# The first stage of a two-block transformer: modulation products in quarters of the array's columns, x times norm on VectorE, another order of weights

## The chip, the cores and the metric

The kernel runs on one core of a Trainium2 chip. The metric is the device time of one execution in microseconds (us), the median of several. The core has TensorE (PE in the rows: matrix products, with its weight loads as PEld), VectorE (DVE), ScalarE (ACT) and GpSimd (POOL); SyncE (SP) only starts transfers here. Each engine works through its own instructions in order, and waits at one of them until what it reads is there and what it writes is free.

## The reference

Everything is fp32. Two transformer blocks on 512 rows of width 1024 follow each other. The change is in the first few lines of the first block, where the input is normalised and modulated before any projection:

```python
m  = jax.nn.silu(c) @ w_mod[l] + b_mod[l]          # c: 1 x 1024, w_mod: 1024 x 6144
sh1, sc1, g1, sh2, sc2, g2 = jnp.split(m, 6, axis=-1)
mc = jax.nn.silu(c_ctx) @ w_mod[l] + b_mod[l]      # the same weights, the context's vector
csh1, csc1, ... = jnp.split(mc, 6, axis=-1)
h  = rms_norm(x, norm1_g[l])  * (1.0 + sc1)  + sh1  # 512 x 1024
hc = rms_norm(xc, norm1_g[l]) * (1.0 + csc1) + csh1 # 256 x 1024
gq, gk, gv, nq, nk, nv, fu, cu, gl = jnp.split(h @ w_in, PROJ_SPLITS, axis=-1)
```

`h` feeds all projections of the token mixer (a convolution branch from `cu`, a Fourier branch from `fu`, a neighbourhood attention from `nq, nk, nv`, a grouped attention), then come a mixture of experts and the second block, which the change does not touch.

## The kernel before, in words

Activations lie transposed: 1024 features as 8 chunks k of 128 partitions, 512 rows in the free dimension. A large product is made in three passes so that it keeps fp32 accuracy: ScalarE casts a raw weight tile (`wraw`, 512 KB) to `whi`, VectorE makes `wlo` = raw - hi, and TensorE adds hi*hi, lo*hi and hi*lo. A projection job of 128 output columns is 8 chunks times 3 matmuls = 24 matmuls of 128x512.

The first stage, in `mixers` (from line 934) and the functions it starts, does this:

- `silu_c` makes silu of the two vectors c and c_ctx (`csil`, and its hi and lo parts `cparts`).
- `jobs_mod`/`mod_job`: the 2048 columns of w_mod that hold shift and scale are 4 groups g of 512; each group comes in 4 transfers kq (`mraw`, 512 KB, two chunks k each). The first transfer of a group is multiplied as it is (native fp32, two matmuls, which the trace shows as four records); the other three are split into `mod_hi` (ScalarE) and `mod_lo` (VectorE) and multiplied in four matmuls each against `cparts`. At the end of a group VectorE copies the sum from the bank to `m`, four small matmuls by `pairs` turn it into columns, and VectorE adds the bias and forms `A` = (1 + scale) * gain. Event `mod0` to `mod3` then stands for group 0 to 3; group g serves the chunks 2g and 2g+1 of h.
- `modulated`: squares and sums of x, the reciprocal root (`xr`), a broadcast over partitions by four transposes, a copy of it to `xbc` on ScalarE, and x times `xbc` on GpSimd chunk by chunk. `modulated_chunk` then makes `h_hi` and `h_lo` of a chunk with that chunk's `A` and shift on ScalarE and VectorE. The same function makes `hc` from ctx.
- `conv_first` is the first projection: three weights `win` (units of the convolution branch) are worked on together, two chunks k of each in turn, 72 matmuls. After it come five more jobs of the convolution, then the Fourier branch's first job.

The order of all instructions comes from a scheduler written in Python. Each piece of work is a generator that names the engine that it wants next and what it needs; `Net.run` always takes the piece that a modelled clock says can start first, with a small bonus for its priority. Transfers of a `stream` are issued ahead as far as a ring of raw tiles reaches. In `mixers` three streams are queued one after the other: `mod_a` (groups 0 and 1, 8 transfers), `jobs0` (the three `win` weights, behind a hold until mod_a's transfers are issued), and `mod_b` (groups 2 and 3, behind a hold until those of jobs0 are). They share one ring of 6 raw tiles. All instructions are recorded by one helper, so the line in the rows is L341 everywhere, and tiles are told apart by their names.

Later in the block, `modulation_rest` computes the other 4096 columns of `m` on VectorE, a multiply-add (`macc`) for each half of a 256 KB transfer (`mw`); its pieces stand between the neighbourhood attention's, whose value tiles `nv` come back from DRAM in 18 transfers on SP's queue.

Of the kernel before, what the change touches and what calls it, by code (L numbers as in the profile page):

```python
# [196 lines left out]
PE, ACT, DVE, POOL, SP = "pe", "act", "dve", "pool", "sp"  # L197
# [191 lines left out]
class Net:  # L389
# [345 lines left out]
    def silu_c(self):  # L735

        nc = self.nc
        self.csil = self.keep.tile([128, 8, 4], F32, name="csil")
        nc.gpsimd.memset(self.csil, 0.0)
        self.cparts = self.keep.tile([128, 8, 4], F32R, name="cparts")  # L740
        self.pairs = self.keep.tile([4, 2], F32, name="pairs")
        self.mod1 = self.keep.tile([128, 16, 2], F32, name="mod1")
        self.A1 = self.keep.tile([128, 8, 2], F32, name="A1")
        self.mod2 = self.keep.tile([128, 4, 8], F32, name="mod2")
        cv = self.vec("cvec").rearrange("p (k c) -> p k c", k=8)
        yield ACT, cv
        c = self.csil[:, :, :2]
        nc.scalar.activation(c, cv, AF.Tanh, scale=0.5)
        yield DVE, c
        nc.vector.scalar_tensor_tensor(c, c, 1.0, cv, op0=OP.add, op1=OP.mult)  # L750
        nc.vector.tensor_scalar(c, c, 0.5, None, op0=OP.mult)
        nc.vector.tensor_tensor(self.pairs, self.ident[:4, :2], self.ident[:4, 2:4], op=OP.add)
        yield from self.split(self.cparts[:, :, 0:2], self.cparts[:, :, 2:4], c)
        self.mark("cparts", self.cparts, c)

    def jobs_mod(self, a, after=None):
        if after:
            yield [], partial(self.hold, after)
        for g in range(2 * a, 2 * a + 2):
            for kq in range(4):  # L760
                yield [(self.T["wmod1"][g, kq], 2, 512, kq == 0)], partial(self.mod_job, g, kq)

    def mod_job(self, g, kq, w):

        nc = self.nc
        if kq == 0:
            yield PE, self.banks, "cparts"
            self.modp = self.banks.take()
        p = self.modp
        for k in range(2):  # L770
            for z, v in enumerate(w):
                c = self.csil if len(w) == 1 else self.cparts
                nc.tensor.matmul(p[:4, :], c[:, kq * 2 + k], v[:, k], start=kq + k + z == 0,
                                 stop=(kq, k, z) == (3, 1, len(w) - 1))
        if kq < 3:
            return
        yield TAIL
        yield DVE, p, self.m512
        m = self.m512.take()
        nc.vector.tensor_copy(m, p[:4, :])  # L780
        self.banks.drop(p)
        yield PE, m, self.banks
        pt = self.banks.take()
# [16 lines left out]
    def modulated(self, pool, x, nt, v, hi, lo, name):  # L800

        nc = self.nc
        n = nt * 128
        sq = self.ring(pool, 2, [128, n], F32, name + "sq")
        acc = pool.tile([128, n], F32, name=name + "acc")
        for k in range(8):
            yield from self.square(acc, x[:, k], sq, k == 0)
        r = self.keep.tile([128, nt], F32, name=name + "r")
        yield from self.column_sums(r, acc, nt, 1024)
        bc = pool.tile([128, n], F32, name=name + "bc")  # L810
        yield from self.row_bcast(bc, r, nt)
        for k in range(8):
            yield POOL, bc
            nc.gpsimd.tensor_tensor(x[:, k], x[:, k], bc, op=OP.mult)
        for k in range(8):
            self.spawn(self.modulated_chunk(k, x[:, k], v, hi[:, k], lo[:, k], f"{name}{k}"), 1, name)
        yield DVE, *(f"{name}{k}" for k in range(8))
        self.mark(name, hi, lo)

# [16 lines left out]
    def modulation_rest(self, ws, accs):  # L836

        nc = self.nc
        for u in range(16):
            yield DVE, accs  # L840
            acc = accs.take()
            for h in range(4):
# [3 lines left out]
                for i in range(2):  # L846
                    k = 2 * h + i
                    yield DVE, w
                    c = self.csil[:, k, 0:1]
# [84 lines left out]
    def mixers(self):  # L934
# [9 lines left out]
        with ExitStack() as e1:  # L944
# [3 lines left out]
                nc.sync.dma_start(self.x[:, 2 * i:2 * i + 2], T["xT"][:, 2 * i:2 * i + 2])  # L948
            nc.scalar.dma_start(self.blk, T["k_blk"])
            nc.scalar.dma_start(self.perm, T["k_perm"])  # L950
            rings = self.ring(pool, 6, [128, 1024], F32, "mraw1"), self.pair_ring(pool, 3, [128, 1024], "mod1")
            self.m512 = self.ring(pool, 2, [4, 512], F32, "m512")
            self.conv_setup()
            self.spawn(self.silu_c(), 0, "silu_c")
            self.spawn(self.modulated(pool, self.x, 4, 0, *self.h, "x"), 1, "x")
            self.stream(self.jobs_mod(0), 6, "mod_a", rings, prio=0)
            self.stream(self.jobs0(), 2, "jobs0")
            self.stream(self.jobs_mod(1, "jobs0 loaded"), 6, "mod_b", rings, prio=0)
            self.until("mod_b loaded")
            self.until("mod3")  # L960
            nc.scalar.dma_start(ctx, T["ctxT"])
# [48 lines left out]
        self.project_out(es, yps)  # L1010

    def jobs0(self):
        yield [], partial(self.hold, "mod_a loaded")
        yield sum((self.win(18 + i) for i in range(FIRST)), []), self.conv_first

    def jobs1(self):
# [2209 lines left out]
```

## Time and profile before

| | |
|---|---|
| median of 3 runs | 2446.87 us (2443.91 to 2449.58) |
| the profiled execution | 2445.25 us, of which 2443.5 us are its span |
| TensorE, busy | 2360.6 us, 97% of the span |
| VectorE, busy | 1674.2 us, 69% |
| ScalarE, busy | 1215.4 us, 50% |
| GpSimd, busy | 160.8 us, 7% |
| moved by DMA | 323.79 MB, mean 133 GB/s |

TensorE is busy nearly all the time, so what an edit is worth has to be looked for where TensorE is idle or runs at its lower clock. In the first 10 us it has no work at all; in the 50 us after that it is busy, but partly with the modulation products and at half clock for some of the time. A row of the timeline gives the start, the length of one instruction or of a merged run of them, the engine (a q behind it: its queue of transfers), what is written and read, how many instructions, and in brackets the idle time ahead of it with what ended it.

### The profile page before, as it was taken

To read this page: it belongs to the slowest core of one execution; us is meant where nothing else is said; L and a number is where in the kernel's file an instruction comes from. 1 tells how busy PE (TensorE), PEld (TensorE's weight loads), DVE (VectorE), ACT (ScalarE), POOL (GpSimd) and SP (SyncE) were. 2 spreads that over 40 slices of the span, in tenths; PEclk is the share of its full clock that TensorE was granted. 3 is DMA by queue.
4 is the path that set the end of the run, shared out by engine and by line. 5 is a ranking of instruction groups with operands and counts; after the bars stand their busy time and mean duration, and the time that the engine had idled before them with its cause. 6 is when DMAs were issued, how large, how long until landed. Compare 5 with 4: busy or idle time off the path is not lost.

```text
span 2443.5 us, 33458 instructions
## 1 busy us (share of the span) xinstructions
PE 2360.6 (97%) x12332; PEld 1940.4 (79%) x12332; DVE 1674.2 (69%) x3138; ACT 1215.4 (50%) x2077; POOL 160.8 (7%) x179
## 2 busy tenths in 40 slices
PE   7999899999997999999999999999999999999998
PEld 3789777888886788887878788888887777888886
DVE  6997577689456989798997752444569975533443
ACT  5433366467443777685546843332343575432333
POOL 3100122100002100002000000000000000000000
PEclk9999999999997999999999999999999999999999
DMA  6223444432262998974221132222222121222231
GB/s 253 97 70 104 131 123 128 148 112 78 74 249 100 397 370 339 341 284 162 78 70 57 35 112 95 95 95 96 100 96 95 49 70 61 95 95 95 95 101 55
DMA packets 104907, 323.79 MB, mean 133 GB/s; under 512 B 12850, under 2 KB 19922, under 8 KB 104612
## 3 DMA queue, kind: packets, MB, share of 16 engines
q1 hardware_dynamic: 91284, 285.40, 33.2%
q0 software_dynamic: 8560, 25.01, 3.6%
q10 hardware_dynamic: 4896, 11.22, 1.2%
q8 instruction: 98, 1.61, 0.3%
q14 instruction: 69, 0.57, 0.1%
HBM read 308.45 MB, written 13.11 MB: 132 GB/s over the span
## 4 chain that ended last, share of the span: by engine, by line
PE 34%; issue 14%; DVE 5%; ACT 1%; DMA 0%; POOL 0%; ACTq 0%; POOLq 0%; DVEq 0%
PE bank L341 34%; DVE G L341 1%; DVE wlo L341 1%; DVE mt L341 1%; DVE sel L341 0%; DVE cP L341 0%; DVE m L341 0%; ACT cP L341 0%; DMA mraw<-yg,dest 0%; ACT whi L341 0%; DVE g_lo L341 0%; ACT G L341 0%; ACT g_hi L341 0%; DVE x L341 0%; POOL rl L341 0%
## 5 line engine op out<-in xcount | busy, mean ns | idle before, releaser
L341 ACT CAST whi<-wraw 128x1024 fp32r<-128x1024 f32 (+1 forms) x321 | 321.0, 1005 | 641.3 <-PE bank L341 599.9
L341 DVE TENSOR_TENSOR wlo<-wraw,whi 128x1024 fp32r<-128x1024 f32 (+1 forms) x321 | 376.2, 1175 | 129.8 <-ACT whi L341 128.8
L341 PE MATMUL bank<-g_hi,whi 128*128 128x512 f32 x992 | 396.1, 399 | 1.8 <-ACT g_hi L341 1.8
L341 PE MATMUL bank<-g_lo,whi 128*128 128x512 f32 x992 | 387.8, 391 | 2.8 <-DVE g_lo L341 2.8
L341 PE MATMUL bank<-g_hi,wlo 128*128 128x512 f32 x992 | 387.9, 391 | 1.1 <-DVE wlo L341 1.1
L341 PEld LDWEIGHTS bank<-g_lo,whi 128*128 128x128 f32 x992 | 186.7, 188 | 43.8 <-DVE g_lo L341 4.7
L341 PE MATMUL bank<-h_hi,wlo 128*128 128x512 f32 x528 | 209.9, 398 | 11.4 <-DVE wlo L341 11.4
L341 PEld LDWEIGHTS bank<-g_hi,whi 128*128 128x128 f32 x992 | 186.5, 188 | 43.3 <-issue 5.1
L341 PEld LDWEIGHTS bank<-g_hi,wlo 128*128 128x128 f32 x992 | 186.5, 188 | 41.7 <-DVE wlo L341 1.9
L341 PE MATMUL bank<-h_hi,whi 128*128 128x512 f32 x528 | 214.5, 406 | 2.1 <-ACT whi L341 2.1
L341 PE MATMUL bank<-h_lo,whi 128*128 128x512 f32 x528 | 208.3, 394 | 0.1
L341 PE MATMUL bank<-u_hi,whi 128*128 128x512 f32 x512 | 202.4, 395 | 0.0
L341 PE MATMUL bank<-u_hi,wlo 128*128 128x512 f32 x512 | 200.8, 392 | 0.0
L341 PE MATMUL bank<-u_lo,whi 128*128 128x512 f32 x512 | 198.9, 388 | 0.0
L341 DVE SCALAR_TENSOR_TENSOR mu<-bank,rbc 128x512 f32<-128x512 f32 x64 | 43.9, 691 | 162.2 <-PE bank L341 155.8
L341 ACT CAST whi<-mraw 128x1024 fp32r<-128x1024 f32 x101 | 105.9, 1049 | 57.8 <-PE bank L341 29.4
L341 DVE TENSOR_TENSOR wlo<-mraw,whi 128x1024 fp32r<-128x1024 f32 x101 | 121.1, 1222 | 17.1 <-ACT whi L341 15.2
L341 PEld LDWEIGHTS bank<-h_hi,wlo 128*128 128x128 f32 x528 | 100.4, 190 | 36.4 <-DVE wlo L341 14.7
L341 PEld LDWEIGHTS bank<-h_hi,whi 128*128 128x128 f32 x528 | 100.8, 191 | 24.1 <-ACT whi L341 2.5
L341 PEld LDWEIGHTS bank<-h_lo,whi 128*128 128x128 f32 x528 | 100.8, 191 | 19.3 <-issue 0.5
L341 PEld LDWEIGHTS bank<-u_hi,wlo 128*128 128x128 f32 x512 | 96.1, 188 | 22.5
L341 PEld LDWEIGHTS bank<-u_lo,whi 128*128 128x128 f32 x512 | 96.2, 188 | 21.2
(541 smaller groups left out, 4827.1 us busy)
## 6 DMA issues: line engine op xcount, KB each, us to landing
mraw<-in_wgu SPq DMA_DIRECT2D x106, 512.0 KB
wraw<-in_win SPq DMA_DIRECT2D x102, 512.0 KB
wraw<-in_wdn SPq DMA_DIRECT2D x78, 512.0 KB
wraw<-in_wup SPq DMA_DIRECT2D x64, 512.0 KB
mraw<-in_wdn SPq DMA_DIRECT2D x50, 512.0 KB
mw<-in_wmod SPq DMA_DIRECT2D x64, 256.0 KB
wraw<-in_wout SPq DMA_DIRECT2D x24, 512.0 KB
wraw<-in_wgu SPq DMA_DIRECT2D x22, 512.0 KB
```

Of the source, the lines that this page charges most:

```text
L341: r = f(*args, **kw)
```

## The change

The diff, cut to its core:

```diff
-        self.csil = self.keep.tile([128, 8, 4], F32, name="csil")
+        self.csil = self.keep.tile([128, 46], F32, name="csil")
...
-        nc.vector.tensor_tensor(self.pairs, self.ident[:4, :2], self.ident[:4, 2:4], op=OP.add)
-        yield from self.split(self.cparts[:, :, 0:2], self.cparts[:, :, 2:4], c)
+        nc.vector.tensor_reduce(self.pairs, self.ident.rearrange("p (q v) -> p v q", q=4)[:, :2], axis=AX.X, op=OP.add)
...
-                yield [(self.T["wmod1"][g, kq], 2, 512, kq == 0)], partial(self.mod_job, g, kq)
+                yield [(self.T["wmod1"][g, kq], 2, 512, True)], partial(self.mod_job, g, kq)
...
         for k in range(2):
-            for z, v in enumerate(w):
-                c = self.csil if len(w) == 1 else self.cparts
-                nc.tensor.matmul(p[:4, :], c[:, kq * 2 + k], v[:, k], start=kq + k + z == 0,
-                                 stop=(kq, k, z) == (3, 1, len(w) - 1))
+            c = 2 * kq + k
+            q = 32 * (c % 4)
+            nc.tensor.matmul(p[q:q + 32, :], self.csil[:, 2 * c:2 * c + 32], w[0][:, k], start=c < 4, stop=c >= 4)
...
-        nc.vector.tensor_copy(m, p[:4, :])
+        nc.vector.tensor_copy(m, p)
...
-        bc = pool.tile([128, n], F32, name=name + "bc")
-        yield from self.row_bcast(bc, r, nt)
+        yield PE, self.banks, r
+        bc = self.banks.take()
+        for j in range(nt):
+            nc.tensor.transpose(bc[:, j * 128:(j + 1) * 128], r[:, j:j + 1].to_broadcast([128, 128]), self.ident)
         for k in range(8):
-            yield POOL, bc
-            nc.gpsimd.tensor_tensor(x[:, k], x[:, k], bc, op=OP.mult)
-        for k in range(8):
+            yield DVE, bc
+            nc.vector.tensor_tensor(x[:, k], x[:, k], bc[:, :n], op=OP.mult)
...
-            rings = self.ring(pool, 6, [128, 1024], F32, "mraw1"), self.pair_ring(pool, 3, [128, 1024], "mod1")
-            self.m512 = self.ring(pool, 2, [4, 512], F32, "m512")
+            raws = self.ring(pool, 8, [128, 1024], F32, "mraw1")
+            self.m512 = self.ring(pool, 2, [128, 512], F32, "m512")
...
-            self.stream(self.jobs_mod(0), 6, "mod_a", rings, prio=0)
+            self.stream(self.jobs_mod((0,)), 8, "mod_a", (raws, None), prio=0)
             self.stream(self.jobs0(), 2, "jobs0")
-            self.stream(self.jobs_mod(1, "jobs0 loaded"), 6, "mod_b", rings, prio=0)
+            self.stream(self.jobs_mod((1, 2, 3)), 8, "mod_b", (raws, None), prio=0)
```

All 16 transfers of w_mod's first part are now multiplied as they are. Chunk c goes to quarter c mod 4 of the array's columns: 32 columns of `csil` from column 2c on are the stationary side (the first two are chunk c's, the others give rows that are not used), and the sum lands in 32 partitions of the bank from 32 * (c mod 4) on; `pairs` adds the four quarters. The casts and subtractions of w_mod are gone, with `cparts`, `mod_hi` and `mod_lo`. x (and ctx) times its norm is done by VectorE, which reads the broadcast from the bank; the copy of it on ScalarE is gone. The streams are group 0, then the three `win` weights, then groups 1 to 3, with no holds, in a ring of 8 raw tiles.

What the scheduler makes of it differs from the kernel before in about the first quarter of the program, up to the router of the mixture of experts. Three places matter below.

TensorE, from the last modulation products to the first matmuls of `conv_first` (`h_hi`, `h_lo` are the parts of h; `ident,xr` are the broadcast's transposes). Before:

```order
L341 MATMUL bank_69<-mod_hi_138,cparts 4x512
L341 MATMUL bank_69<-mod_lo_141,cparts 4x512
L341 MATMUL bank_71<-pairs,m_143 128x2 x4
L341 MATMUL bank_72<-mraw_132,csil 4x512 x2
L341 MATMUL bank_73<-h_hi,whi_101 128x512
L341 MATMUL bank_73<-h_lo,whi_101 128x512
L341 MATMUL bank_73<-h_hi,wlo_104 128x512
```

Now:

```order
L341 MATMUL bank_70<-mraw_135,csil 32x512 x2
L341 MATMUL bank_70<-mraw_136,csil 32x512 x2
L341 MATMUL bank_70<-mraw_137,csil 32x512 x2
L341 MATMUL bank_71<-ident,xr 128x128 x4
L341 MATMUL bank_72<-pairs,m_138 128x2 x4
L341 MATMUL bank_73<-pairs,m_139 128x2 x4
L341 MATMUL bank_66<-pairs,m_138 128x2 x4
L341 MATMUL bank_68<-pairs,m_139 128x2 x4
L341 MATMUL bank_67<-h_hi,whi_101 128x512
L341 MATMUL bank_67<-h_lo,whi_101 128x512
L341 MATMUL bank_67<-h_hi,wlo_104 128x512
```

Before, the transposes stood far ahead and `conv_first` began between the modulation groups; now the transposes, then all four groups' `pairs`, stand between the last modulation product and `conv_first`, which then runs in one piece.

ScalarE, at the end of `conv_first` (`ct` is the first step of what follows a convolution unit, one for each of the three units; `whi_101<-wraw_100` is the cast of the weight of the next job). Before:

```order
L341 ACTIVATE ct_145<-bank_73 128x512
L341 ACTIVATE hcsq_396<-ctx 128x256
L341 CAST whi_101<-wraw_100 128x1024
L341 ACTIVATE hcsq_397<-ctx 128x256
L341 ACTIVATE ct_146<-bank_67 128x512
L341 CAST whi_102<-wraw_97 128x1024
```

Now:

```order
L341 ACTIVATE ct_142<-bank_71 128x512
L341 CAST hc_hi<-ctx 128x256
L341 ACTIVATE ct_143<-bank_72 128x512
L341 CAST whi_101<-wraw_100 128x1024
L341 CAST whi_102<-wraw_97 128x1024
L341 CAST whi_103<-wraw_98 128x1024
```

The cast for the next job stood between the first and the second unit's `ct`; it now stands behind the third's.

VectorE, and then SP, where the neighbourhood attention starts (`wlo_106<-wraw_98` is the lo part of a weight that TensorE waits for in the trace of before). VectorE before:

```order
L341 TENSOR_TENSOR wlo_106<-wraw_97,whi_103 128x1024
L341 TENSOR_SCALAR macc_1900<-mw_1898,csil 128x256
L341 SCALAR_TENSOR_TENSOR macc_1900<-mw_1898,csil,macc_1900 128x256
L341 TENSOR_TENSOR wlo_106<-wraw_98,whi_103 128x1024
L341 SCALAR_TENSOR_TENSOR nqs<-bank_70,nqs 64x128 x8
L341 TENSOR_TENSOR wlo_104<-wraw_99,whi_101 128x512
L341 SCALAR_TENSOR_TENSOR macc_1900<-mw_1899,csil,macc_1900 128x256 x2
```

Now:

```order
L341 TENSOR_TENSOR wlo_106<-wraw_97,whi_103 128x1024
L341 TENSOR_SCALAR macc_1828<-mw_1826,csil 128x256
L341 SCALAR_TENSOR_TENSOR macc_1828<-mw_1826,csil,macc_1828 128x256
L341 SCALAR_TENSOR_TENSOR macc_1828<-mw_1827,csil,macc_1828 128x256
L341 SCALAR_TENSOR_TENSOR nqs<-bank_70,nqs 64x128 x5
L341 TENSOR_TENSOR wlo_106<-wraw_98,whi_103 128x1024
L341 SCALAR_TENSOR_TENSOR nqs<-bank_70,nqs 64x128 x3
```

A third `macc`, which reads the second transfer `mw_1827`, and five of the eight `nqs` now stand ahead of that `wlo`. SP before:

```order
L341 DMA wraw_98<-in_win 128x1024
L341 DMA nv_1910<-nvd 128x1x128 x8
L341 DMA nv_1910<-nvd 128x2x128
L341 DMA nv_1911<-nvd 128x1x128 x8
L341 DMA nv_1911<-nvd 128x2x128
L341 DMA wraw_99<-in_wbranch 128x512
L341 DMA mw_1898<-in_wmod 128x512
L341 DMA wraw_100<-in_win 128x1024
L341 DMA mw_1899<-in_wmod 128x512
```

Now:

```order
L341 DMA wraw_98<-in_win 128x1024
L341 DMA mw_1826<-in_wmod 128x512
L341 DMA wraw_99<-in_wbranch 128x512
L341 DMA nv_1838<-nvd 128x1x128 x8
L341 DMA nv_1838<-nvd 128x2x128
L341 DMA nv_1839<-nvd 128x1x128 x8
L341 DMA nv_1839<-nvd 128x2x128
L341 DMA wraw_100<-in_win 128x1024
L341 DMA mw_1827<-in_wmod 128x512
```

The first `mw` and a `wbranch` weight moved ahead of the 18 transfers of `nv`; the second `mw` stays behind them, now with a `win` weight of 512 KB directly ahead of it.

## Rows read from the trace of the kernel before

**Rows 1.** Busy time by stretch: TensorE, weight loads, VectorE, ScalarE, GpSimd, granted clock, DMA.

```profile
30.00:35.00 5.00, 3.37 (x10) 2.00 (x11) 4.62 (x6) 0.57 (x1) 5.00 (x3) 0.53 0.26 99
95.00:100.00 5.00, 4.13 (x11) 3.16 (x11) 3.63 (x4) 2.47 (x3) 0.00 (x0) 0.52 0.76 256
260.00:270.00 10.00, 0.96 (x5) 0.46 (x3) 1.84 (x3) 0.62 (x1) 0.74 (x2) 0.79 0.67 189
```

**Rows 2.** Transfers from 0 to 60 us: GB/s in slices of 1.5 us.

```profile
GB/s 0 147 317 377 372 379 421 423 410 412 410 410 292 355 401 410 429 401 421 360 330 0 0 0 0 33 318 71 341 377 412 393 156 14 0 5 235 431 33 0
```

**Rows 3.** Timeline of SP's queue: the modulation's transfers.

```profile
2.88 12.97 SPq L341 DMA_DIRECT2D mraw<-in_wmod  x8
...
17.89 22.99 SPq L341 DMA_DIRECT2D mraw<-in_wmod  x8
```

**Rows 4.** Timeline of TensorE in the first stage.

```profile
11.15 3.57 PE L341 MATMUL bank<-mraw,csil 128*4 128x512 f32 x4 [11.15 <-DVE xacc L341]
...
18.80 1.12 PE L341 MATMUL bank<-ident,xr 128*128 128x128 f32 x4 [0.56 <-POOL xr L341]
...
21.84 1.88 PE L341 MATMUL bank<-mraw,csil 128*4 128x512 f32 x4
...
31.63 1.86 PE L341 MATMUL bank<-pairs,m 4*128 4x2 f32 x8 [1.96 <-DVE m L341]
```

**Rows 5.** Timeline of TensorE: native products that use 64 columns each.

```profile
1224.63 1.08 PE L341 MATMUL bank<-mt,vr 128*64 128x512 f32 x4
```

**Rows 6.** Page, costliest groups: a VectorE operation that reads a bank.

```profile
L341 DVE SCALAR_TENSOR_TENSOR mu<-bank,rbc 128x512 f32<-128x512 f32 x64 | 43.9, 691 | 162.2 <-PE bank L341 155.8
```

**Rows 7.** Timeline of VectorE: operations of the same size, alone and beside GpSimd.

```profile
36.91 1.29 DVE L341 TENSOR_TENSOR h_lo<-x,h_hi 128x512 fp32r<-128x512 f32 x2
...
51.01 0.17 DVE L341 TENSOR_TENSOR mod<-bank,vecs 128x8 f32<-128x8 f32 x1 [0.30 <-PE bank L341]
...
73.72 5.84 DVE L341 SCALAR_TENSOR_TENSOR ca<-cz,vecs,ca 128x512 f32<-128x512 f32 x5
...
195.68 5.35 DVE L341 SCALAR_TENSOR_TENSOR ca<-cz,vecs,ca 128x512 f32<-128x512 f32 x7
```

**Rows 8.** Timeline of GpSimd: x times its norm.

```profile
20.62 15.97 POOL L341 TENSOR_TENSOR x<-x,xbc 128x512 f32<-128x512 f32 x8 [1.87 <-ACT xbc L341]
```

**Rows 9.** Timeline of TensorE where conv_first ends and the next job starts.

```profile
63.60 0.39 PE L341 MATMUL bank<-h_hi,wlo 128*128 128x512 f32 x1
63.83 0.39 PE L341 MATMUL bank<-h_hi,whi 128*128 128x512 f32 x1
```

**Rows 10.** Timeline of ScalarE at the same place.

```profile
62.11 1.04 ACT L341 CAST whi<-wraw 128x1024 fp32r<-128x1024 f32 x1
...
65.10 0.59 ACT L341 ACTIVATE ct<-bank 128x512 f32<-128x512 f32 x1
```

**Rows 11.** Timeline of VectorE at the same place.

```profile
63.18 1.23 DVE L341 TENSOR_TENSOR wlo<-wraw,whi 128x1024 fp32r<-128x1024 f32 x1 [0.51 <-ACT whi L341]
```

**Rows 12.** Timeline of TensorE at the first Fourier job.

```profile
94.37 0.50 PE L341 MATMUL bank<-h_hi,whi 128*128 128x512 f32 x1 [2.12 <-ACT whi L341]
...
95.97 0.79 PE L341 MATMUL bank<-h_hi,wlo 128*128 128x512 f32 x1 [0.87 <-DVE wlo L341]
...
103.93 0.40 PE L341 MATMUL bank<-h_hi,whi 128*128 128x512 f32 x1
```

**Rows 13.** Timeline of SP's queue: the value tiles of the neighbourhood attention.

```profile
245.42 16.24 SPq L341 DMA_DIRECT2D nv<-nvd  x18
```

**Rows 14.** Timeline of VectorE behind them.

```profile
268.12 0.35 DVE L341 TENSOR_SCALAR macc<-mw,csil 128x256 f32<-128x256 f32 x1 [17.71 <-DMA mw<-in_wmod]
268.91 1.22 DVE L341 TENSOR_TENSOR wlo<-wraw,whi 128x1024 fp32r<-128x1024 f32 x1
...
270.79 0.28 DVE L341 SCALAR_TENSOR_TENSOR nqs<-bank,nqs 64x128 fp32r<-64x128 f32 x1 [0.34 <-ACT nqs L341]
```

**Rows 15.** Timeline of TensorE at the same place.

```profile
270.19 0.79 PE L341 MATMUL bank<-h_hi,wlo 128*128 128x512 f32 x1 [9.22 <-DVE wlo L341]
```

More of the change, by code (lines that the diff above doesn't have):

```diff
@@ L737, in silu_c @@
         nc = self.nc
-        self.csil = self.keep.tile([128, 8, 4], F32, name="csil")
+        self.csil = self.keep.tile([128, 46], F32, name="csil")
         nc.gpsimd.memset(self.csil, 0.0)
-        self.cparts = self.keep.tile([128, 8, 4], F32R, name="cparts")
-        self.pairs = self.keep.tile([4, 2], F32, name="pairs")
+        self.pairs = self.keep.tile([128, 2], F32, name="pairs")
         self.mod1 = self.keep.tile([128, 16, 2], F32, name="mod1")
@@ L746, in silu_c @@
         yield ACT, cv
-        c = self.csil[:, :, :2]
+        c = self.csil[:, :16].rearrange("p (k c) -> p k c", k=8)
         nc.scalar.activation(c, cv, AF.Tanh, scale=0.5)
@@ L751, in silu_c, with jobs_mod @@
         nc.vector.tensor_scalar(c, c, 0.5, None, op0=OP.mult)
-        nc.vector.tensor_tensor(self.pairs, self.ident[:4, :2], self.ident[:4, 2:4], op=OP.add)
-        yield from self.split(self.cparts[:, :, 0:2], self.cparts[:, :, 2:4], c)
[L754 to L759, printed above, removed]
+        nc.vector.tensor_reduce(self.pairs, self.ident.rearrange("p (q v) -> p v q", q=4)[:, :2], axis=AX.X, op=OP.add)
+        self.mark("csil", c, self.pairs)
+    def jobs_mod(self, groups):
+        for g in groups:
             for kq in range(4):
-                yield [(self.T["wmod1"][g, kq], 2, 512, kq == 0)], partial(self.mod_job, g, kq)
+                yield [(self.T["wmod1"][g, kq], 2, 512, True)], partial(self.mod_job, g, kq)
     def mod_job(self, g, kq, w):
@@ L766, in mod_job @@
         if kq == 0:
-            yield PE, self.banks, "cparts"
+            yield PE, self.banks, "csil"
             self.modp = self.banks.take()
@@ L809, in modulated @@
         yield from self.column_sums(r, acc, nt, 1024)
-        bc = pool.tile([128, n], F32, name=name + "bc")
-        yield from self.row_bcast(bc, r, nt)
+        yield PE, self.banks, r
+        bc = self.banks.take()
+        for j in range(nt):
+            nc.tensor.transpose(bc[:, j * 128:(j + 1) * 128], r[:, j:j + 1].to_broadcast([128, 128]), self.ident)
         for k in range(8):
-            yield POOL, bc
-            nc.gpsimd.tensor_tensor(x[:, k], x[:, k], bc, op=OP.mult)
-        for k in range(8):
+            yield DVE, bc
+            nc.vector.tensor_tensor(x[:, k], x[:, k], bc[:, :n], op=OP.mult)
             self.spawn(self.modulated_chunk(k, x[:, k], v, hi[:, k], lo[:, k], f"{name}{k}"), 1, name)
+        self.banks.drop(bc)
         yield DVE, *(f"{name}{k}" for k in range(8))
@@ L848, in modulation_rest @@
                     yield DVE, w
-                    c = self.csil[:, k, 0:1]
+                    c = self.csil[:, 2 * k:2 * k + 1]
                     if k == 0:
@@ L1012, in jobs0 @@
     def jobs0(self):
-        yield [], partial(self.hold, "mod_a loaded")
         yield sum((self.win(18 + i) for i in range(FIRST)), []), self.conv_first
```

## The prediction, made blind

> **What bounds the kernel now.** I read the page's busy shares first: TensorE works 97% of the span, so time is to be won only where it idles or runs at half clock. The list of waits then names its few long stops, and the timeline of each engine around them says what ended each. For this change three places count: the first 64 us, the first Fourier job, and the start of the neighbourhood attention.
>
> In the first stage the first transfer of w_mod is used at 11.15 us [rows 4], and from there to about 31 us the queues move some 410 GB/s almost without a break [rows 2]. So the stage is bound by its transfers, not by the casts and subtractions that the change removes. GpSimd takes 15.97 us for x times its norm, 2.0 us a chunk [rows 8], but beside those transfers. TensorE was out of work for 1.96 us before the second group's `pairs`, and these then ran at half clock: 1.86 us [rows 4], granted clock 0.53 between 30 and 35 us [rows 1]. The first matmul after `conv_first` starts at 63.83 us, 0.23 us behind the one before it [rows 9]; this is the point that I measure the new stage against.
>
> At the first Fourier job TensorE waits 2.12 us for a cast and 0.87 us for a subtraction [rows 12], then runs at a granted clock of 0.52 [rows 1]. At the neighbourhood attention it idles 9.22 us for `wlo` [rows 15]: VectorE has stood 17.71 us at a `macc` whose transfer [rows 14] is queued behind 18 others that take SP 16.24 us [rows 13].
>
> **The first stage, step by step.** Removed: 12 casts on ScalarE, 12 subtractions on VectorE and 48 split products on TensorE. The 16 transfers and the three `win` weights are the same bytes, in another order. In the kernel before, groups 2 and 3 were spread up to 41 us, since SP had to wait for raw tiles (the second run of eight takes 22.99 us to issue, the first 12.97) [rows 3]; now nothing holds them for long, and all 19 come in one piece. One transfer of 512 KB at 410 GB/s is 1.28 us; 18 more behind the first are 23.0 us: the last lands at 34.2 us.
>
> A transfer's two native products, four records, take 1.88 us on the full array [rows 4]. Two quarters may work at the same time: four records of the same length with 64 columns each took 1.08 us [rows 5]. At 1.08 they keep up with the transfers, and the last ends at 35.2 us. While the clock is low at the start (3.57 us for four records [rows 4]) TensorE falls behind by a transfer or so, and catches up at full clock before 34 us.
>
> The Trainium skill, PSUM — Partial Sum Buffer (Engine vs sequencer instructions), says that matmuls start and complete in program order. By it the quarters would win nothing, each transfer would cost the full-array price, and the stage would be TensorE's; rows 5 speak against it for halves, no row shows quarters. The Trainium skill, TensorEngine Tiling (Array Packing) (Key Properties), says that different tiles can load weights and multiply in parallel, which those rows bear out for two. The rule of program order is priced as rival 1 below.
>
> Then the new chain, none of it beside TensorE work:
> - four transposes, 1.12 us [rows 4]: 36.3 us. Before, they stood early and GpSimd worked off x beside the transfers; now they stand behind all modulation products.
> - x times norm on VectorE out of the bank, eight times between 0.645 (two such operations from SBUF in 1.29 us [rows 7]) and 0.691 us (an operation that reads a bank [rows 6]); I take 0.66, 5.3 us: 41.6 us.
> - bias and `A` for groups 0 and 1, four small ones at 0.17 [rows 7], 0.7 us: 42.3 us; a copy of group 2's sum, now 128 rows, at the bank price 0.69: 43.0 us.
> - TensorE has then idled 6.7 us, three times what gave half clock before. Two `pairs` at 1.86 each [rows 4]: `conv_first` starts at 46.7 us.
> - 72 matmuls at 0.228 us [rows 9], 16.4 us; half clock until about 49 us (before it was gone some 6 us after the restart), 2.4 us at half speed, costs 1.2 us; the sums and transposes of the context now stand inside this piece, 0.5 us that the kernel before spends later, and they wait some 0.6 us for GpSimd (the same chain of x waited 0.56 [rows 4]). End: 65.4 us.
>
> Less the 0.5 us, that is 1.1 us later than before. So half a hundred products less on TensorE give nothing: they lay beside transfers, while VectorE's 7 us now lie bare.
>
> **The cast behind the third `ct`.** As the rows of ScalarE in the part on the change show, the next job's `whi` was cast between the tails (from 62.11 us [rows 10]), with `wlo` at 63.18 us [rows 11], just in time. Now it waits for the third unit: 0.1 us, `ct` 0.5 of its 0.59, cast 1.04 [rows 10], so TensorE idles 1.6 us; `wlo` 1.23 us later [rows 11] less two matmuls, another 0.8 us. Together 2.4 us. Whether the clock falls: a gap of 1.96 us was followed by half clock, and 2.12 plus 0.87 us too; I take it as at the Fourier job, where the 22 matmuls from 95.97 to 103.93 us took 7.96 instead of 5.0 us [rows 12]: 2.9 us. Bounds 0 and 2.9.
>
> **The first Fourier job.** VectorE does the context's product itself, without a copy: eight operations of 256 columns, at most 0.69 each [rows 6], in place of GpSimd's, beside which its taps ran at 1.17 us (5.84 for five) against 0.76 alone (5.35 for seven) [rows 7]. ScalarE and VectorE reach the casts of the Fourier tables that much earlier, and with them the raw tiles come free for that job's weight. With five convolution jobs in between, some 27 us, the weights are there. The job's loss, 2.12 us ahead of it and 9.56 us (94.37 to 103.93) instead of 5.5 for its 24 matmuls, goes: 6.2 us gained. Of this 0 would be left if the tables came as late as before.
>
> **The neighbourhood attention.** One `mw` moves ahead of the `nv` transfers, but VectorE now also waits for the second, which is behind them and behind a `win` of 512 KB instead of a `wbranch` of 256 KB: 0.64 us later at 410 GB/s, so at 268.8 us instead of 268.1 [rows 14]. Behind it, ahead of `wlo`, stand one `macc` (0.4) and five `nqs`, each of which waits for ScalarE, 0.62 us from one to the next (the `wlo` ends at 270.13 us, the second `nqs` starts at 270.79, having waited 0.34 us for ScalarE [rows 14]), 3.1 us. `wlo` then starts at 272.3 instead of 268.91: 3.4 us later; three matmuls more stand ahead of the wait: 2.7 us net. Lower bound: the `macc` doesn't wait and the 9.2 us fall to what five `nqs` leave, -5; upper, the second transfer lands a few us later still, +6.
>
> **The stretch after it** has the same jobs in a slightly other order. No row prices that; the bounds are the longest wait there once less or once more, 9.2 us either way [rows 15]. I take 0, and 4 for the range.
>
> **Sum.** First stage +1.1, cast +2.4, clock behind it +2.9, Fourier job -6.2, attention +2.7: +2.9 us. On the profiled execution's 2445.25 us that is 2448.2; this execution is 1.6 us below the median of 2446.87, so against the median 2449.8. I round down to 2449, as two of the terms take the clock's loss in full.
>
> **Rivals.**
> 1. The quarters work one after the other (slower). Place: the products from 11 to 35 us. Each transfer costs 1.88 us, above the transfers' 1.28: 13 of them behind a slow start to 20 us end at 44.5 us, 9.3 us later than 35.2. It decides from the point where a transfer's products take over 1.28 us. The time is 2458. For it: no row has quarters. Against: rows 5.
> 2. The clock holds and the second `mw` is early (faster). The gap of 1.6 us doesn't lower the clock (-2.9), `pairs` and `conv_first` run at full clock (-1.9 and -1.2), and the attention's wait is as before (-2.7): 8.7 us less than forecast, 2440. For it: 1.6 us is shorter than either gap that lowered the clock [rows 4, 12]. Against: 6.7 us of idle time ahead of `pairs` is more than any gap that did.
> 3. VectorE's queue at the attention (slower). If the second `mw` lands after 270 us, or another `macc` stands ahead of a `wlo` later, each such wait is paid by TensorE in full, as the 9.22 us were: some 5 to 7 us on top, 2455. It decides where a `macc` starts after 270 us.
> 4. The change does its work, but only beside transfers, and neither the Fourier job's wait nor the others move: +1.1 alone, 2448. This falls within the forecast's own range.
>
> **Chances.** What a measurement of this kernel can tell from no change is 0.2%, 4.9 us: 2442.0 to 2451.8. The forecast with rival 4 has 0.5 (own range 2444 to 2454, of which a small part lies above the bound), rival 1 0.12, rival 2 0.2, rival 3 0.18. So faster 0.2, same 0.46, slower 0.34, and a range of 2439 to 2459.
>
> **What would show it.** First stage: no gap in the transfers until 34 us; a transfer's four records within 1.1 us; VectorE's eight products of x in 5.3 us; the first matmul of `conv_first` near 46.7 us at half clock. Cast: a gap of about 1.6 and one of 0.8 us on TensorE around 65 to 68 us. Fourier: no wait over 1 us there. Attention: one wait for `wlo` of about 12 us. The forecast is wrong if `conv_first` starts before 43 or after 50 us, if the wait at the attention is gone, or if new waits of some us appear between 270 and 520 us.

## The result, and the profile after

| | before | after |
|---|---|---|
| median of 4 runs | 2445.57 us (2443.91 to 2449.58) | 2461.84 us (2460.05 to 2463.63) |
| the profiled execution, its span | 2445.25 us, 2443.5 us | 2460.05 us, 2458.3 us |

The ratio is 1.0068, with an interval of 1.0056 to 1.0080: the changed kernel is slower by 16 us, and its time lies above the range of 2439 to 2459 us. The profile's busy shares say little. TensorE has lost 1.7 us of busy time (it had 2360.6 us), VectorE 14, ScalarE 12 and GpSimd 23, and the span is 14.8 us longer:

```profile
PE 2358.9 (96%) x12332; PEld 1937.0 (79%) x12332; DVE 1660.3 (68%) x3144; ACT 1203.1 (49%) x2059; POOL 138.0 (6%) x163
```

**The first stage** goes nearly as the prediction drew it. The transfers of the kernel after, 0 to 60 us in slices of 1.5 us, go on to 37 us without the dip at 18 us and the break behind 31 us of [rows 2]:

```profile
GB/s 0 147 306 383 376 402 418 423 418 412 410 401 421 407 407 412 392 410 401 415 407 415 407 401 330 3 0 0 44 268 388 0 0 0 0 5 0 0 0 0
```

TensorE after, in the first 70 us (start, duration, operation, count; in brackets the idle time ahead and what ended it); these answer [rows 4] and [rows 9]:

```profile
10.96 5.67 PE L341 MATMUL bank<-mraw,csil 128*32 128x512 f32 x16 [10.96 <-DMA mraw<-in_wmod]
...
33.98 1.05 PE L341 MATMUL bank<-mraw,csil 128*32 128x512 f32 x4 [0.23 <-DMA mraw<-in_wmod]
34.97 0.65 PE L341 MATMUL bank<-ident,xr 128*128 128x128 f32 x4
35.45 1.84 PE L341 MATMUL bank<-pairs,m 128*128 128x2 f32 x16
41.73 3.57 PE L341 MATMUL bank<-pairs,m 128*128 128x2 f32 x16 [4.43 <-DVE m L341]
45.16 0.77 PE L341 MATMUL bank<-h_hi,whi 128*128 128x512 f32 x1
...
67.99 0.71 PE L341 MATMUL bank<-h_hi,whi 128*128 128x512 f32 x1 [2.71 <-ACT whi L341]
...
69.25 0.79 PE L341 MATMUL bank<-h_hi,wlo 128*128 128x512 f32 x1
```

A transfer's four records take 1.05 us, then TensorE waits 0.23 us for the next transfer. After the last, VectorE's work lies bare: eight products of x in 4.87 us and a copy, while TensorE idles 4.43 us ahead of the second group of `pairs`, which run at half clock (granted 0.50, 1.2 of 2.4 GHz). The cast comes 2.71 us late. VectorE after, at the same place [rows 7]:

```profile
35.65 4.87 DVE L341 TENSOR_TENSOR x<-x,bank 128x512 f32<-128x512 f32 x8 [10.18 <-PE bank L341]
...
40.99 1.28 DVE L341 COPY m<-bank 128x512 f32<-128x512 f32 x2
```

**The Fourier job and the attention.** The kernel after by stretch (length; TensorE, weight loads, VectorE, ScalarE, GpSimd; granted clock, DMA share, GB/s): TensorE is busy without a break and at full clock from 75 to 125 us, around the Fourier job, where it had run at half clock from 95 us on [rows 1], and the 3 us of waits [rows 12] are gone. The second row is for the stretch that follows the attention's start.

```profile
75.00:125.00 50.00, 50.00 (x255) 42.58 (x254) 47.53 (x74) 19.54 (x33) 0.00 (x0) 1.00 0.30 103
...
280.00:745.00 465.00, 448.18 (x2770) 373.76 (x2770) 329.82 (x803) 256.57 (x568) 58.68 (x80) 0.99 0.39 128
```

At the attention SP's run of 18 transfers starts 1.2 us earlier and takes 1.0 us less than in [rows 13], the kernel after:

```profile
244.18 15.20 SPq L341 DMA_DIRECT2D nv<-nvd  x18
```

So VectorE's `macc`, though it reads the second `mw`, starts at 266.27 us, 1.85 us ahead of the one in [rows 14]; then come the five `nqs`, as forecast (VectorE after):

```profile
266.27 0.48 DVE L341 SCALAR_TENSOR_TENSOR macc<-mw,csil,macc 128x256 f32<-128x256 f32 x1 [15.22 <-DMA mw<-in_wmod]
...
269.78 1.23 DVE L341 TENSOR_TENSOR wlo<-wraw,whi 128x1024 fp32r<-128x1024 f32 x1
```

TensorE resumes at 271.06 us, 0.87 us later than in [rows 15]. Up to here the kernel after has lost next to nothing.

**Where the time went.** In the stretch from 280 to 745 us, to which the prediction gave 0, TensorE was idle 8.75 us before (465 less the 456.25 in the next row, the kernel before), and 16.8 us after (465 less the 448.18 above):

```profile
280.00:745.00 465.00, 456.25 (x2829) 381.27 (x2828) 334.39 (x809) 257.62 (x572) 56.94 (x80) 1.00 0.41 131
```

The largest new wait is one of 3.88 us, TensorE after:

```profile
332.46 0.28 PE L341 MATMUL bank<-nkd_hi,nqs 128*128 128x256 f32 x1
...
334.25 0.28 PE L341 MATMUL bank<-nkd_lo,nqs 128*128 128x256 f32 x1
338.41 2.79 PE L341 MATMUL bank<-ident,nP 128*128 128x128 f32 x12 [3.88 <-DVE rden L341]
```

Sixteen scores (`nkd,nqs`) are followed at once by the transposes of their softmax (`nP`). Between the two VectorE and ScalarE work through row maxima, exponentials and sums; meanwhile TensorE has nothing else to do: its own order has no projection between the two, and VectorE splits the next weight only after the softmax, its `wlo` starts at 338.45 us. The same twelve transposes in the kernel before, TensorE:

```profile
331.34 0.39 PE L341 MATMUL bank<-y_hi,whi 128*128 128x512 f32 x1
...
336.77 0.39 PE L341 MATMUL bank<-h_hi,wlo 128*128 128x512 f32 x1
337.00 1.47 PE L341 MATMUL bank<-ident,nP 128*128 128x128 f32 x12
```

There 24 projection matmuls (12 with `y`, 12 with `h`) fill the 5.66 us, and the transposes wait for nothing; after, they run at half clock as well (2.79 against 1.47 us). The list of waits for 280 to 735 us says the same in sums. TensorE after, what it waited for, us in total, times, longest:

```profile
PE bank L341 <- DVE rden L341: 5.9, 2, 3.9
PE bank L341 <- DVE wlo L341: 3.0, 4, 1.3
...
PE bank L341 <- ACT P L341: 2.0, 3, 1.3
PE bank L341 <- ACT nP L341: 1.9, 4, 0.8
```

and before:

```profile
PE bank L341 <- DVE rden L341: 2.3, 2, 1.7
PE bank L341 <- DVE wlo L341: 1.5, 3, 1.0
```

The router's first sum marks the end of the stretch. TensorE before, then after:

```profile
749.97 1.36 PE L341 MATMUL bank<-ones,ssq 128*128 128x1 f32 x8 [0.78 <-ACT ssq L341]
```

```profile
761.83 1.05 PE L341 MATMUL bank<-ones,ssq 128*128 128x1 f32 x8 [0.78 <-ACT ssq L341]
```

So the 14.8 us of the span are 0.9 up to 271 us, 11.0 from there to the router, 2.9 behind it.

### The profile page after: what moved, and what is told of

Its sections match the earlier page's. It is cut to its first block, busy times and chain, and to the rows that moved or that the text cites. A ratio compares the mean times of both kernels' runs of the same rounds, so it can differ in the third digit from the quotient of the medians.

```text
span 2458.3 us, 33402 instructions
## 1 busy us (share of the span) xinstructions
PE 2358.9 (96%) x12332; PEld 1937.0 (79%) x12332; DVE 1660.3 (68%) x3144; ACT 1203.1 (49%) x2059; POOL 138.0 (6%) x163
## 4 chain that ended last, share of the span: by engine, by line
PE 33%; issue 14%; DVE 5%; ACT 1%; DMA 0%; POOL 0%; ACTq 0%; POOLq 0%; DVEq 0%
PE bank L341 33%; DVE G L341 1%; DVE wlo L341 1%; DVE mt L341 1%; DVE cP L341 0%; DVE sel L341 0%; DVE m L341 0%; DMA mraw<-yg,dest 0%; ACT cP L341 0%; ACT whi L341 0%; DVE g_lo L341 0%; ACT G L341 0%; DVE x L341 0%; DVE nm L341 0%; POOL rl L341 0%
```

## The experiments

The theory: the first stage itself is worth about nothing, and the loss comes from the order of the work between 271 and 762 us, which the scheduler drew anew because the first stage ended at another modelled time. The rival: the new stage leaves something behind (a later start, other buffers, other traffic) that slows what follows.

To part the two, the order has to be held while the code changes. The scheduler's choices of one kernel were recorded as a list (piece of work, step), and another kernel follows that list:

```diff
         while not cond():
-            best = None
+            best = self.follow()         # the piece that the list names next, if it can run
+            if best is not None:
+                self.forward(best[2])
+                continue
+            best = None                  # else the scheduler's own choice
```

The recorded choices between ScalarE and VectorE (`lighter`) are followed too. Where the list begins is one line in `mixers`.

**1. The new stage, then the order of before.**

```diff
             self.until("x", "hc", "first")
+            self.plan = load_plan()      # recorded in the kernel before
```

> The changed first stage, and from there on (once h, hc and conv_first are issued) every step in the order of the kernel before, given by a list in place of the scheduler's choice; ScalarE-or-VectorE choices too. Theory 1: the 16 us are lost behind 270 us, by the other order of the same work. Then this kernel is within 4 us of the kernel before: 2446 to 2450 (first stage +1.1, cast +2.4, clock +2.9, Fourier job -6.2, no extra wait at the attention). Theory 2: something that the new stage leaves behind (placement of tiles and banks, transfers) slows what follows: then it stays near the changed kernel, 2458 to 2463.

Measured: 2444.26 us, ratio 1.0000 [0.9990, 1.0009], 2 us below the range of theory 1. From `conv_first`'s end on all is in the old order, and the whole loss is gone, though the cast is still late. TensorE:

```profile
66.43 0.50 PE L341 MATMUL bank<-h_hi,whi 128*128 128x512 f32 x1 [2.71 <-ACT whi L341]
...
266.42 0.79 PE L341 MATMUL bank<-h_hi,wlo 128*128 128x512 f32 x1 [8.19 <-DVE wlo L341]
...
747.00 1.32 PE L341 MATMUL bank<-ones,ssq 128*128 128x1 f32 x8 [0.78 <-ACT ssq L341]
```

**2. The old stage, then the order of after.** The kernel before with the same line, the list recorded in the kernel after.

> The first stage of the kernel before, and from there on every step in the order of the changed kernel. Theory 1: the later order carries the loss: 2456 to 2462. Theory 2: 2444 to 2450.

Measured: 2470.41 us, 1.0095 [1.0080, 1.0110]. It loses without the change, and more than the change did and than theory 1 allowed: a wait of 8.19 us at 104 us comes on top, which no other kernel has. There the list puts 15 steps of the convolution (`ca`, 10.02 us) ahead of the Fourier job's `wlo` on VectorE, which behind the old stage is at that point only at 92.89 us. The scores again stand bare. VectorE, then TensorE:

```profile
92.89 10.02 DVE L341 SCALAR_TENSOR_TENSOR ca<-cz,vecs,ca 128x512 f32<-128x512 f32 x15
...
104.11 0.79 PE L341 MATMUL bank<-h_hi,wlo 128*128 128x512 f32 x1 [8.19 <-DVE wlo L341]
...
347.81 2.79 PE L341 MATMUL bank<-ident,nP 128*128 128x128 f32 x12 [4.34 <-DVE rden L341]
```

**3. The new stage and its own order up to the end of the convolution's jobs, some 220 us; then the order of before.** This leaves everything that the rival blames in place.

```diff
         self.until("y3", "nvd0", "nvd1", "zeros")
+        self.plan = load_plan()          # recorded in the kernel before
```

> The changed kernel with its own order of steps up to the end of the convolution's jobs (some 220 us), and from there the order of the kernel before, word for word on all engines. Theory (the 11 us between 271 and 762 us come from the order of that stretch alone): the scores of three attention units are again followed by 24 projection matmuls ahead of their transposes, no TensorE wait over 2.5 us between 280 and 745 us, the router's ones,ssq at 749 to 752 us instead of 761.8, median 2449 to 2452, ratio 1.001 to 1.003. Rival (what the first 220 us leave behind carries it: the later start, the DMA queues, the raw tiles): ones,ssq at 758 or later and 2458 to 2462 as in the changed kernel. If the attention's wait grows to about 12 us as forecast, both are 2.5 us later.

Measured: 2445.33 us, 1.0006 [0.9997, 1.0015], 16.5 us less than the kernel after (15 by the ratios), and below the 2449 to 2452 that the theory gave. TensorE:

```profile
266.82 0.79 PE L341 MATMUL bank<-h_hi,wlo 128*128 128x512 f32 x1 [6.63 <-DVE wlo L341]
...
334.55 1.47 PE L341 MATMUL bank<-ident,nP 128*128 128x128 f32 x12
...
745.41 1.05 PE L341 MATMUL bank<-ones,ssq 128*128 128x1 f32 x8 [0.78 <-ACT ssq L341]
```

The transposes wait for nothing again, and the attention's wait is 6.63 instead of 9.57 us: what that one has over 6.63 us is order as well. The rival falls.

**4 and 5. A push of 1 us on the modelled clock,** in the kernel before and in the kernel after, with nothing else changed:

```diff
             self.until("y2")
+            self.clk.at[PE] += 1.0
```

> The kernel before in all its code, but the scheduler's modelled time of TensorE is put 1 us later at one point (when the Fourier branch is done), so that it orders the neighbourhood attention and what follows otherwise. Theory 1 in its wider form, that any such reshuffle costs or wins several us: 3 us or more away from the kernel before, either way. If the changed kernel's order is bad for a reason of its own: within 2 us of the kernel before.

> The changed kernel with its own scheduling, but the scheduler's modelled time of TensorE is put 1 us later when the Fourier branch is done (the same nudge as in old_stage_nudged). If the changed kernel's 16 us are one draw of an order that any small shift redraws, this one lands elsewhere: 5 us or more away from the changed kernel, most likely between 2444 and 2456. If the order that the scheduler finds behind this first stage is bad by its nature: within 3 us of 2462.

Measured: before with the push 2448.95 us, 1.0015 [1.0006, 1.0023]; after with it 2459.21 us, 1.0058 [1.0041, 1.0075]. The first loses 3.8 us, a little over the 3 us that the wider theory asked for. The second is no test: the push left the order from 271 to 800 us as it was, and the trace repeats the wait of 3.89 us at the same transposes.

**6 and 7. The same push a little later,** behind `self.until("y3", "nvd0", "nvd1", "zeros")`, which does move that stretch:

> The kernel before with the same nudge at the same place; its order differs from there on at 71 places on TensorE. With old_stage_nudged this gives the spread that reshuffles of the stretch alone make: 2441 to 2456 by theory 1, and within 2 us of the kernel before if order hardly matters.

> The changed kernel with its own scheduling; the scheduler's modelled time of TensorE is put 1 us later just before the neighbourhood attention is set up. Up to there the order is the changed kernel's, behind it it differs at 61 places on TensorE (new_stage_nudged left the order of that stretch as it was, and so was no test of it). Theory 1, the loss sits in one order of that stretch: the 3.9 us wait for the softmax near 338 us goes or moves, and the time is 2444 to 2456. If the stretch is slow behind the new stage whatever its order: within 3 us of 2462.

Measured: the kernel before, pushed, 2457.23 us, 1.0050 [1.0036, 1.0064]: it loses 12 us, just more than the 2441 to 2456 expected, with not an instruction of the first stage changed, and with the same sign, transposes behind their own scores. The kernel after, pushed, is at 2452.55 us, 1.0035 [1.0021, 1.0048], so it wins back 9; a wait of that kind, 2.65 us, is left at 388 us. TensorE of the kernel before, pushed:

```profile
384.74 0.28 PE L341 MATMUL bank<-nkd_lo,nqs 128*128 128x256 f32 x1
388.39 2.79 PE L341 MATMUL bank<-ident,nP 128*128 128x128 f32 x12 [3.37 <-DVE rden L341]
```

From the first matmul after the attention's wait to the router's `ones,ssq`, by the order that was followed there (in experiment 4 that wait stands at another place):

| order of the stretch | stage | us |
|---|---|---|
| of before | old (the kernel before) | 479.78 |
| of before | new: experiments 1, 3, 8, 9, 10, 11, 12 | 480.58, 478.59, 481.57, 479.92, 479.02, 480.61, 480.39 |
| of after | new: the kernel after, experiment 5 | 490.77, 491.32 |
| of after | old: experiment 2 | 491.82 |
| redrawn | old: 6, new: 7 | 489.09, 485.36 |

Whichever stage stands ahead, the old order takes 478.6 to 481.6 us and the new one 490.8 to 491.8.

The other five ask what the first stage is worth when the order behind it is held to that of before.

**8. The cast early.** As 1, with the cast `whi` for the next job ahead of the first `ct` on ScalarE, and its `wlo` two steps earlier on VectorE (two entries of the list moved).

> As new_stage_old_order, but the cast of the next job's weight stands on ScalarE ahead of the first unit's ct, and its subtraction on VectorE two steps ahead of where it was; nothing else moves. If the wait behind the third ct and the half clock after it cost what was forecast (2.4 and 2.9 us), TensorE has no wait near 65 us and this kernel is 4 to 5.5 us faster than new_stage_old_order. If the clock falls for the idle time before conv_first anyway, only 2.4.

Measured: 2439.97 us, 0.9977 [0.9968, 0.9986]; 4.3 us less than 1 (5.6 by the ratios), where 4 to 5.5 were expected. Of the waits at 66 us 0.55 us is left, the clock stays up, though `conv_first` still starts at half clock (the second row here has one matmul in 0.77 us). TensorE:

```profile
41.68 3.57 PE L341 MATMUL bank<-pairs,m 128*128 128x2 f32 x16 [4.43 <-DVE m L341]
45.11 0.77 PE L341 MATMUL bank<-h_hi,whi 128*128 128x512 f32 x1
65.53 0.50 PE L341 MATMUL bank<-h_hi,wlo 128*128 128x512 f32 x1 [0.55 <-DVE wlo L341]
```

**9. One quarter in place of four,** on top of 8:

```diff
-            nc.tensor.matmul(p[q:q + 32, :], self.csil[:, 2 * c:2 * c + 32], w[0][:, k], start=c < 4, stop=c >= 4)
+            nc.tensor.matmul(p[:32, :], self.csil[:, 2 * c:2 * c + 32], w[0][:, k], start=c == 0, stop=c == 7)
```

> new_stage_old_order_early_cast with all modulation products in the first 32 columns, one after the other (same order of everything, 32 rows copied to m instead of 128). If the quarters work side by side, this takes the price of one native product after the other, 1.76 to 1.88 us a transfer instead of 1.05 and above the 1.28 of the transfers: the products end near 41 to 44 us instead of 35, and the kernel is 6 to 9 us slower than new_stage_old_order_early_cast (2446 to 2449). If quarters run one after the other anyway: no difference.

Measured: 2446.28 us, 1.0008 [0.9998, 1.0017], 6.3 us more than 8 (7.6 by the ratios). TensorE no longer waits for transfers, and ends them later:

```profile
21.49 20.79 PE L341 MATMUL bank<-mraw,csil 128*32 128x512 f32 x48
...
48.95 3.57 PE L341 MATMUL bank<-pairs,m 32*128 32x2 f32 x16 [4.22 <-DVE m L341]
```

The 48 records are 12 transfers' worth, 1.73 us each: above the 1.28 us that a transfer takes. The second `pairs` start 7.3 us later.

**10. x times norm on GpSimd again,** on top of 8 (a copy of the broadcast to SBUF on ScalarE, the products on GpSimd).

> new_stage_old_order_early_cast with x times norm on GpSimd again, out of a copy on ScalarE, everything else in the same order. By the length of the step (16 us against 5.3 on the path): conv_first starts 10 us later, 2450. By what each chunk needs (GpSimd hands over a chunk every 2.0 us, TensorE takes 2.05 us for one, and VectorE is free at once for the two copies of m): conv_first starts some 3 us earlier, near 42 us, and the kernel is 1 to 4 us faster than new_stage_old_order_early_cast, 2436 to 2439.

Measured: 2441.42 us, 0.9986 [0.9974, 0.9997], 1.4 us more than 8, with intervals that overlap. Neither what I hoped (1 to 4 us less) nor a large loss: GpSimd takes 11 us for the eight where VectorE took 4.87, but `pairs` need not wait for them (39.33 instead of 41.68 us), and only the first `h_lo` is late. What `conv_first` wins by starting 2.3 us earlier it loses again: 1.30 us of wait, and a clock that stays at 0.50 until 52 us, where in 8 it is at 1.00 from 50 us on. GpSimd and TensorE of this kernel:

```profile
36.17 11.04 POOL L341 TENSOR_TENSOR x<-x,xbc 128x512 f32<-128x512 f32 x8 [15.51 <-ACT xbc L341]
39.33 3.57 PE L341 MATMUL bank<-pairs,m 128*128 128x2 f32 x16 [2.18 <-DVE m L341]
46.12 0.79 PE L341 MATMUL bank<-h_lo,whi 128*128 128x512 f32 x1 [1.30 <-DVE h_lo L341]
```

**11. The broadcast beside the transfers.** The bare chain stands behind all products only because of the priorities; so, on top of 8:

```diff
-            self.m512 = self.ring(pool, 2, [128, 512], F32, "m512")
-            self.spawn(self.modulated(pool, self.x, 4, 0, *self.h, "x"), 1, "x")
-            self.stream(self.jobs_mod((0,)), 8, "mod_a", (raws, None), prio=0)
+            self.m512 = self.ring(pool, 4, [128, 512], F32, "m512")
+            self.spawn(self.modulated(pool, self.x, 4, 0, *self.h, "x"), -1, "x")
+            self.stream(self.jobs_mod((0,)), 8, "mod_a", (raws, None), prio=2)
```

(likewise for `mod_b`; and the scheduler's cost of a 32-column product is halved).

> The changed first stage with other priorities in the scheduler: x's chain ahead of everything on TensorE, the modulation's streams behind the ends of their groups, four tiles for m instead of two, and products of 32 columns counted at half their modelled time; from there on the order of the kernel before and the early cast. Transposes, VectorE's eight products and each group's pairs then lie beside the transfers, and conv_first begins between the modulation products. If VectorE's bare 5 us, the late pairs and the half clock before conv_first are what the new stage lost, conv_first ends near 53 us instead of 65, and the kernel is 6 to 12 us faster than new_stage_old_order_early_cast: 2428 to 2434. If the later stages are bound by transfers that don't start earlier, less than 3 us of it are left.

Measured: 2435.70 us, 0.9964 [0.9950, 0.9979], 4.3 us less than 8, where 6 to 12 were expected. x is ready at 23.3 us, but `conv_first` now runs between the products, from 28.5 us on, and ends at about 60 instead of 53 us. The transfers are not held up by it: the last of the 16 is issued at 28.9 us, as in 12.

**12. The same with the full cost,** which keeps the products ahead of `conv_first`.

> As early_broadcast, but the modulation products stay ahead of conv_first (the scheduler counts a product of 32 columns in full again), so that no transfer is held up by matmuls in between; cast and subtraction of the next job's weight early, and then the order of the kernel before. The transfers end near 34 us without a break, conv_first runs from 36 to 54 us at full clock, and the kernel is 4 to 8 us faster than early_broadcast: 2428 to 2432. If what follows waits for transfers instead (weights of the next job, ctx), it stays at 2434 to 2437.

Measured: 2434.61 us, 0.9956 [0.9942, 0.9969]: the fastest of all, 10.8 us under the kernel before and 27 under the kernel after, though not to be told from 11, and short of the 2428 to 2432 that I expected. It lies in the 2434 to 2437 that I gave for the case that what follows waits for transfers; no run shows whether that is the reason. TensorE:

```profile
17.29 1.12 PE L341 MATMUL bank<-ident,xr 128*128 128x128 f32 x4
...
25.27 3.23 PE L341 MATMUL bank<-mraw,csil 128*32 128x512 f32 x16
30.46 1.06 PE L341 MATMUL bank<-pairs,m 128*128 128x2 f32 x8 [1.96 <-DVE m L341]
...
36.78 1.91 PE L341 MATMUL bank<-mraw,csil 128*32 128x512 f32 x12
38.62 0.50 PE L341 MATMUL bank<-h_hi,whi 128*128 128x512 f32 x1
...
255.01 0.80 PE L341 MATMUL bank<-h_hi,wlo 128*128 128x512 f32 x1 [8.08 <-DVE wlo L341]
```

`conv_first` starts at 38.6 instead of 45.1 us (experiment 8) and at full clock; TensorE leaves the attention's wait 6.9 us earlier than in 8, and 11.4 earlier than in 1.

## Why the prediction was wrong

The step that failed is "The stretch after it has the same jobs in a slightly other order ... I take 0, and 4 for the range." It measured 11.0 us. For the same work, from the attention's wait to the router, TensorE was idle 17.6 instead of 9.5 us, 8 us more, and busy 473.2 instead of 470.3 us, 2.9 more, at a granted clock of 0.96 from 320 to 360 us and 0.97 from 400 to 450, where before it was 1.00. The prediction had named a bound, 9.2 us either way, which the loss passed, and had put only 4 of it into the range. Rival 3 put 5 to 7 us about there, but for another cause. Experiments 1, 2 and 3 show that this order alone, with either stage, makes the difference; 4 and 6 show that the kernel before stood on a good draw: the kernels with the four other draws of the stretch (after, 4, 6, 7) are all slower than it. That bare softmax chains are the mechanism is read from five traces (after, 2, 5, 6, 7: a wait of 2.65 to 4.34 us for `rden` ahead of twelve transposes); in the kernel before the longest wait for `rden` is 1.7 us. They are the largest part, 3.6 us more waiting for `rden` than before; the rest of the 8 us is many waits of 1.3 us and less. Neither these nor the bare chains were undone one by one, so how the 11 us divide among them is not shown.

The other steps, in their order:

- The first stage: +1.1 forecast. TensorE was done with `conv_first` at 65.28 us (67.99 less the wait), 1.45 later than in [rows 9]; less the 0.5 us of context work inside, +0.95. Right, by terms that partly cancel: the products of x took 4.87 instead of 5.3, the second group of `pairs` began at 41.73 instead of 43.0, TensorE had idled 4.43 instead of 6.7 us (the `pairs` of groups 0 and 1 ran ahead of the gap, the sum had put them behind it), and the half clock of 0.50 lasted from there to 50.8 us. That the size came out so closely has luck in it: in experiment 1, with the same instructions up to there, the half clock ended at 47.7 us, and `conv_first` was done at 63.72 us.
- The cast: 2.4 forecast, 2.71 and 0.3 measured. The clock behind it: 2.9 forecast, about 1.6 measured (eight matmuls at 0.43 instead of 0.23 us). Experiment 8, which takes most of both away, gains 4.3: the measured sum, 4.6, agrees, and the forecast's 5.3 was near it.
- The Fourier job: -6.2 forecast. Ahead of the attention's wait TensorE stands at 261.49 us, 0.52 later than before with three matmuls (0.68) more done, and it has paid a new wait of 0.88 us at 226 us. So the job gave back 0.95 + 4.6 + 0.9 + 0.15, some 6.6 us. Right.
- The attention: +2.7 forecast, +0.35 measured (9.57 against 9.22 us). Here only a size was off: five `nqs` and a `macc` cost the 3.5 us that I had priced, but the second `mw` landed 2.5 us before the 268.8 us that I had taken, as SP's run started earlier and was shorter.
- Behind the router another 2.9 us were lost, which I had not priced. From `ones,ssq` to the end of the span the kernels took from 1691.4 (8) to 1697.5 us (6), with either order: what sets it stays open.

The rivals: 1 was wrong, since a transfer's four records took 1.05 us; experiment 9 builds it and pays 6.3 us, where I had said 9.3. Its price of 1.88 us was not of the full array, as I had it, but of products that all use the same four columns (128*4 in [rows 4]). The Trainium skill, PSUM — Partial Sum Buffer (Engine vs sequencer instructions), says that matmuls start and complete in program order, and I had read that as one after the other. Products on different quarters overlap here; no run shows that they start or complete in another order. 2 was wrong: the clock fell both times; only its last part, the attention's wait as before, came (+0.35). 3 had the right region and sign, but not the mechanism: no `macc` beyond the attention's cost over 1.3 us. The sign that I gave for being wrong, "new waits of some us appear between 270 and 520 us", is what came.

What the change does with the order behind it held is nothing: 1.0000. What it frees (the casts, subtractions, products and the Fourier job's wait) it gives back as 4.4 us of idle TensorE ahead of `pairs`, half clock and a late cast; with these mended, and other priorities for it, it is worth 0.44% (experiment 12).

## What to carry to other kernels

Where a program orders the instructions, an edit at the front is two changes: itself, and a new draw of everything behind it. Price the second by the spread that a push without meaning makes (here -9 to +12 us of 2445), put that into the range, and hold the order fixed before an edit is praised or blamed. In the trace, a wait of the busiest engine behind a chain with none of its own work laid over it (scores, softmax, transposes) is the sign of a bad draw.

## What was not expected of the hardware

- Products on different quarters of the columns overlapped well beyond two. One quarter alone took 1.73 us for a transfer's four records at granted clock 1.00 (experiment 9). In experiment 12, where tiles had piled up, twelve records ran in 1.91 us at 36.78 us, 0.64 for four, at granted clock 1.00 too: 2.7 times as fast. Where only one transfer was there at a time, on two quarters, four records took 1.05 us, 1.65 times as fast.
- Behind many short gaps the granted clock stayed up, behind one longer gap it fell. The kernel after by stretch (length; TensorE; granted clock, DMA share, GB/s): with 0.23 us idle at each transfer it kept the full clock, and behind the gap of 4.43 us it had half of it while it worked without a break.

```profile
24.00:36.00 12.00, 10.11 (x48) 1.00 1.03 406
...
42.00:50.00 8.00, 8.00 (x27) 0.50 0.38 131
```

- How long the half clock lasted changed from one kernel to the next with the same instructions: behind the gap of 4.43 us to 50.8 us (after), 49.1 (experiment 8) and 47.7 (experiment 1).
- GpSimd's products of x took 1.38 us each (11.04 for eight) in experiment 10, where the transfers moved 168 GB/s on average, against 2.0 at 267 GB/s [rows 8]. VectorE was busy most of the time in both, with other operations; what makes the difference stays open.
- The first products ran at half speed though the granted clock reads 1.00 there: in the kernel before, four records took 3.57 us at 11.15 us, as long as the 3.58 us that four such records took at 33.42 us and granted clock 0.50. The prediction called this a low clock; the column alone does not show it.
